# Down projection of a ConvGLU in fp32: every activation sum formed a stage earlier, a seventh raw weight tile, and the fourth weight combination in another order

## The chip, the cores and the metric

The kernel runs on one core of a Trainium2 chip. The metric is device time in microseconds (us) for one execution of the whole program; lower is better. The time before is the median of three runs.

## The reference

One decoder layer and a final norm, all in float32. What the change touches is the last part of the layer, the ConvGLU:

```python
h = rms_norm(x, norm2)
g = causal_dwconv(h @ w_gate)            # 3 taps along the tokens
act = silu(g) * (h @ w_up)
x = x + act @ w_down
```

D_MODEL is 2048, D_FF is 5504 (43 blocks of 128), and there are 512 + 8 x 8 = 576 tokens. Before it stand a norm, one wide input projection, three mixers and an output projection; behind it the final norm. The outputs also hold copies of the caches.

## The kernel before, in words

**Products.** TensorE gets each float32 operand as two rounded halves, hi and lo, and one float32 product is three passes: hi by hi, hi by lo, lo by hi (`product`, L945). A weight tile is split by `split_w`: ScalarE makes the hi half (L933), VectorE subtracts it and leaves the lo half (L934). Three hi and three lo tiles rotate.

**Pairs of blocks.** The 576 tokens are two halves of 288. Both the gate/up stage and the down stage take two output blocks at a time as a 2 x 2 scheme with seven products in place of eight (`strassen_steps`). The weights of a pair come in four raw tiles, b11, b12, b22 and b21. Its products come in the order 11, s1, s2, 12, s3, s4, 22. The names are those of the activation operands. The weight operands are b11; b12 - b11 (formed on VectorE, L990); T2 = b22 - that (VectorE, L998); b21; b22 - b12 (VectorE, L1005); b22; and b21 - T2, the fourth combination, formed on GpSimd (L1009) in b21's own tile. In the up stage a product is 24 matmuls with weight tiles of 128 x 1024 (512 KB), in the down stage 15 matmuls with tiles of 128 x 640 (320 KB). After product 11, ScalarE copies its result (L985), so one L985 is one pair. Results are taken from PSUM by VectorE; in the down stage that is L1487, which adds them to the residual x1.

**Raw weight tiles** come from `raw_tile`, which hands out tiles `wr` and `wx` in turn, three of each. A load waits until the last reader of its tile is done. Loads are issued on SyncE's queue (SP) in program order, and what stands behind a load that waits, waits too.

**The down stage** goes over D_FF in four chunks of ten blocks (NDC = 4, DCHUNK = 5 pairs of blocks), and in each over the 16 output blocks in eight pairs. The activation operands of a chunk must be there as hi and lo halves: 11, s2 and s1 together as s12, 12 and 22 together as own, s4 and s3 together as s34. Each is one piece, 20 pieces for a chunk. They are kept in 28 slots, of which a chunk takes 18. The pieces of the next chunk are made while this one runs (`act_pieces`), each after a step that PIECE_DUE lists; steps are counted over the products of the chunk. Pieces that are left over go between the first products of the next chunk.

**Where the sums come from.** s1, s2, s3 and s4 are sums and differences of the two token halves of two activation blocks. For chunk 0 they are formed in the up stage by `sums` (L1265, L1266, L1271), stored, and loaded again by `first_pieces`. For chunks 1 to 3 the raw activation blocks are loaded to tiles `al` (six of them), and `act_pieces` forms the sums on VectorE itself (L1445, L1446, L1452) between the splits (L1443, L1456; ScalarE L1442, L1453, L1455). The last three blocks of D_FF are handled after chunk 3 (`last_pieces`), without pieces of this kind.

Of the kernel before, what the change touches and what calls it, by code (L numbers as in the profile page):

```python
# [16 lines left out]
P = 128  # L17
# [5 lines left out]
HALF = 288  # L23
# [60 lines left out]
def decoder_step(ctx: ExitStack, tc, I, O):  # L84
# [16 lines left out]
    def nm(s):  # L101
        uid[0] += 1
        return f"{s}_{uid[0]}"
# [798 lines left out]
    wxs = ctx.enter_context(ExitStack())  # L902
    wx = [wxs.enter_context(tc.tile_pool(name="weights2", bufs=1, side="right", reuse_waits="tile")), 1024]
    tps = ctx.enter_context(ExitStack())
# [14 lines left out]
    def work(n=TOK):  # L919
        return wk.tile([P, n], F32, tag="wk", bufs=16, padded_shape=[P, EW], name=nm("wk"))  # L920
# [3 lines left out]
    def raw_tile():  # L924
        rawn[0] += 1
        if rawn[0] % 2:
            return wp.tile([P, 1024], F32, tag="wr", name=nm("wr"))
        return wx[0].tile([P, wx[1]], F32, tag="wx", bufs=3, name=nm("wx"))

# [38 lines left out]
    def strassen_steps(load, X, evac, split, n, urgent=False, late=False):  # L968
# [25 lines left out]
        yield  # L994
        b22 = load(1, 1) if late else b22
        b21 = load(1, 0)
# [23 lines left out]
        with first():  # L1020
            hl = split(w, b21[:, :w])
        product(a, hl, c["22"], False)
# [216 lines left out]
    def state_out(nst, f0, nf):  # L1239
# [4 lines left out]
        for f in range(nf):  # L1244
# [4 lines left out]
    sum_d = [(dp.tile([P, TOK], F32, name=f"s12d{i}"), dp.tile([P, TOK], F32, name=f"s34e{i}"))  # L1249
             for i in range(DCHUNK)]  # L1250
# [33 lines left out]

    def first_pieces(X, n):

        half = [work() for _ in range((n + 1) // 2)]
        for i in range(n):
            j = i % 2 * HALF
            dma(half[i // 2][:, j:j + HALF], act_d[2 * i][:, :HALF])  # L1290

        def load(src):
            t = work()
            dma(t, src)
            return t

        raw = {("s12", i): load(sum_d[i][0]) for i in range(n)}
        yield
        for i in range(n):
            if i % 2 == 0:  # L1300
                t11 = next_slot("11")
            hl = single_of(t11, i % 2)
            src = half[i // 2][:, i % 2 * HALF:(i % 2 + 1) * HALF]
            with_unit(nc.scalar.activation(hl[0], src, AF.Copy))
            nc.vector.tensor_sub(hl[1], src, hl[0].bitcast(F32))
            X.put("11", i, hl)
            yield
        todo = [(c, i) for c in ("s12", "own", "s34") for i in range(n)]
        for c, i in todo:
            if c == "own" and i == 0:  # L1310
                raw.update({("own", k): load(act_d[2 * k + 1]) for k in range(n - 1)})
            if c == "own" and i == n - 1:
                raw.update({("own", n - 1): load(act_d[2 * n - 1])})
                raw.update({("s34", k): load(sum_d[k][1]) for k in range(n)})
            t = next_slot(c)
            src = raw[c, i]
            with_unit(nc.scalar.activation(t[:, 0], src, AF.Copy))
            nc.vector.tensor_sub(t[:, 1], src, t[:, 0].bitcast(F32))
            for name, hl in zip({"s12": ("s2", "s1"), "own": ("12", "22"), "s34": ("s4", "s3")}[c], pair_of(t)):
                X.put(name, i, hl)  # L1320
            yield
# [18 lines left out]
    for nf in GROUPS:  # L1340
# [8 lines left out]
        if f0 == 0:  # L1349
            begun = {0: gate_pair(ht, 0, 0, urgent=True), 2: gate_pair(ht, 2, 2, urgent=True, late=True)}  # L1350
            advance(begun[0][2], 3)
            advance(begun[2][2], 2)
        for f in range(0, nf, 2):
            ff = f0 + f
# [21 lines left out]
            if ups and nf > 1:  # L1376
                for _ in up_steps(*ups.pop(0)):
                    pass
                go_on(len(later))
            if f + 1 < nf:  # L1380
# [4 lines left out]

    nextX = Halves(DCHUNK)
    nxt = first_pieces(nextX, DCHUNK)
    steps = up_steps(*ups.pop(0))
    next(steps)
    next(nxt)  # L1390
    free.extend(n_ for k in RELEASE for n_ in rest[k])
    for n_ in FIRST_PIECES:
# [20 lines left out]

    AL = 6

    def act_tile(k):
        t = fp.tile([P, TOK], F32, tag="al", bufs=AL, name=nm("al"))
        dma_paced(t, act_d[k])
        return t

    def act_pieces(X, k0, n):

        al, t11 = [], {}
        order_ = [(c, i) for i in range(n - 2) for c in ("11", "s12", "own", "s34")]
        order_ += [(c, i) for i in (n - 2, n - 1) for c in ("11", "s12")]
        order_ += [(c, i) for c in ("own", "s34") for i in (n - 2, n - 1)]
        names = {(c, i): free.pop(0) for c, i in order_ if c != "11" or i % 2 == 0}
        for (c, _), name in names.items():
            now.setdefault(c, []).append(name)

        def load():
            if len(al) < n:
                i = len(al)
                al.append((act_tile(k0 + 2 * i), act_tile(k0 + 2 * i + 1)))

        def piece(c, i):
            ae, ao = al[i]
            if c == "11":
                if i % 2 == 0:
                    t11[i // 2] = slot_of(names[c, i])  # L1440
                hl = single_of(t11[i // 2], i % 2)
                with_unit(nc.scalar.activation(hl[0], ae[:, :HALF], AF.Copy))  # L1442
                nc.vector.tensor_sub(hl[1], ae[:, :HALF], hl[0].bitcast(F32))  # L1443
                X.put("11", i, hl)
                nc.vector.tensor_add(ae[:, HALF:], ae[:, HALF:], ao[:, HALF:])  # L1445
                nc.vector.tensor_sub(ae[:, :HALF], ae[:, HALF:], ae[:, :HALF])  # L1446
                return
            t = slot_of(names[c, i])
            src = ae if c == "s12" else ao
            if c == "s34":  # L1450
                s2 = ae[:, :HALF].unsqueeze(1).to_broadcast([P, 2, HALF])
                with_unit(nc.vector.tensor_sub(halves(ao), halves(ao), s2))  # L1452
                nc.scalar.activation(t[:, 0], src, AF.Copy)  # L1453
            else:
                with_unit(nc.scalar.activation(t[:, 0], src, AF.Copy))  # L1455
            nc.vector.tensor_sub(t[:, 1], src, t[:, 0].bitcast(F32))  # L1456
            for name, hl in zip({"s12": ("s2", "s1"), "own": ("12", "22"), "s34": ("s4", "s3")}[c], pair_of(t)):
                X.put(name, i, hl)
            if c == "s34":
                load()  # L1460

        for _ in range(AL // 2):
            load()
        yield
        for c, i in order_:
            piece(c, i)
            yield

# [25 lines left out]
    for ci in range(NDC):  # L1494
# [3 lines left out]
        if ci < NDC - 1:  # L1498
            nextX = Halves(DCHUNK)
            nxt = act_pieces(nextX, f0 + nf, DCHUNK)  # L1500
# [7 lines left out]
        for m in range(0, KD, 2):  # L1508
            def load(h, c, m=m, wv=wv):
                t = raw_tile()  # L1510
                last_w[0] = dma(t[:, :DCHUNK * P].rearrange("p (k c) -> p k c", k=DCHUNK), wv[h][:, :, (m + c) * P:(m + c + 1) * P])
                return t
            pairs.append(strassen_steps(load, X, add_to(m), split_w, DCHUNK, urgent=m < 4,
                                        late=m == 2))
        going, last = last, nxt
# [137 lines left out]
```

## Time and profile before

| | us |
|---|---|
| median of 3 runs (lowest, highest) | 2648.74 (2645.61, 2650.98) |
| the profiled execution | 2641.39 |
| its span in the trace | 2639.5 |
| TensorE busy | 2551.3 (97%) |
| VectorE busy | 1920.6 (73%) |
| ScalarE busy | 972.1 (37%) |
| GpSimd busy | 622.8 (24%) |

The profiled execution is 7.35 us under the median. Its span leaves out 1.9 us around the program. Busy shares are means over stages with different limits.

In the rows below, a window row gives its bounds and length in us, then the busy time and the number of instructions of TensorE (PE), its weight loads (PEld), VectorE (DVE), ScalarE (ACT) and GpSimd (POOL), the granted TensorE clock as a share of full speed, the DMA engines' busy share and GB/s. A timeline row gives start and duration in us, engine, line, operation and out<-in, and in brackets how long the engine had been idle before it and what ended that. A chain row gives start and duration of one piece of the chain that ended last. A group row gives busy us, mean ns of one, and idle us before.
 The up stage lies at about 1140 to 2050 us of the span, the down stage's four chunks at about 2080 to 2570 us.

### The profile page before, as it was taken

To read this page: it belongs to the slowest core of one execution; us is meant where nothing else is said; L and a number is where in the kernel's file an instruction comes from. 1 tells how busy PE (TensorE), PEld (TensorE's weight loads), DVE (VectorE), ACT (ScalarE), POOL (GpSimd) and SP (SyncE) were. 2 spreads that over 40 slices of the span, in tenths; PEclk is the share of its full clock that TensorE was granted. 3 is DMA by queue.
4 is the path that set the end of the run, shared out by engine and by line. 5 is a ranking of instruction groups with operands and counts; after the bars stand their busy time and mean duration, and the time that the engine had idled before them with its cause. 6 is when DMAs were issued, how large, how long until landed. Compare 5 with 4: busy or idle time off the path is not lost.

```text
span 2639.5 us, 48741 instructions
## 1 busy us (share of the span) xinstructions
PE 2551.3 (97%) x19855; PEld 2495.6 (95%) x19855; DVE 1920.6 (73%) x2619; ACT 972.1 (37%) x1445; POOL 622.8 (24%) x460
## 2 busy tenths in 40 slices
PE   8999989989999999999999999999999999989997
PEld 7999889989989999999999999999999998989897
DVE  5667766865766544597878787877777888888875
ACT  6121221222121233354444444444444544444445
POOL 0434334434443000022222121212121111101014
PEclk9999989989999999999999999999999999999999
DMA  8547457537655696556555555555555865555534
GB/s 272 140 122 182 134 148 194 164 110 197 167 152 168 179 281 196 162 181 194 172 185 157 177 153 169 161 166 161 169 162 175 286 183 152 148 147 168 160 100 150
DMA packets 608210, 451.47 MB, mean 171 GB/s; under 512 B 22967, under 2 KB 570082, under 8 KB 601586
## 3 DMA queue, kind: packets, MB, share of 16 engines
q1 hardware_dynamic: 591358, 438.72, 56.0%
q10 hardware_dynamic: 16628, 9.64, 1.2%
q8 instruction: 156, 2.56, 0.4%
q14 instruction: 68, 0.56, 0.1%
HBM read 402.75 MB, written 132.81 MB: 203 GB/s over the span
## 4 chain that ended last, share of the span: by engine, by line
PE 83%; DVE 8%; DMA 6%; issue 1%; ACT 1%; SPq 0%; POOL 0%; DVEq 0%; ACTq 0%
PE a L945 27%; PE acc L176 11%; PE acc L178 10%; PE acc L177 10%; PE pt L945 7%; PE s L945 6%; PE b L945 6%; DMA ev<-in_cache_kv_w_dram 2%; DVE wl L934 2%; DMA al<-act 1%; DVE av L594 1%; DVE xs L1456 1%; DMA wr<-in_w_down_dram 1%; DVE wl L153 1%; PE ps L569 1%
## 5 line engine op out<-in xcount | busy, mean ns | idle before, releaser
L945 PE MATMUL a<-xs,wh 128*128 128x288 f32 x4032 | 814.4, 296 | 14.2 <-ACT wh L933 8.4
L945 PEld LDWEIGHTS a<-xs,wh 128*128 128x128 f32 x4032 | 647.7, 189 | 21.0 <-ACT wh L933 10.7
L176 PE MATMUL acc<-xs,wh 128*128 128x288 f32 x2208 | 663.4, 301 | 0.0
L177 PE MATMUL acc<-xs,wh 128*128 128x288 f32 x2208 | 657.1, 298 | 0.4 <-DVE xs L203 0.3
L178 PE MATMUL acc<-xs,wl 128*128 128x288 f32 x2208 | 655.9, 297 | 0.2 <-DVE wl L153 0.2
L945 PE MATMUL a<-xs,wl 128*128 128x288 f32 x2016 | 592.6, 295 | 1.6 <-DVE wl L934 1.6
L933 ACT ACTIVATE wh<-wr 128x1024 fp32r<-128x1024 f32 (+1 forms) x300 | 276.7, 924 | 519.7 <-PE a L945 210.9
L176 PEld LDWEIGHTS acc<-xs,wh 128*128 128x128 f32 x2208 | 417.5, 189 | 8.4 <-issue 7.6
L178 PEld LDWEIGHTS acc<-xs,wl 128*128 128x128 f32 x2208 | 419.5, 190 | 4.4 <-issue 3.9
L177 PEld LDWEIGHTS acc<-xs,wh 128*128 128x128 f32 x2208 | 418.5, 190 | 1.7 <-DVE xs L200 0.6
L945 PEld LDWEIGHTS a<-xs,wl 128*128 128x128 f32 x2016 | 378.5, 188 | 2.9 <-DVE wl L934 2.7
L1009 POOL TENSOR_TENSOR wx<-wx,wr 128x1024 f32<-128x1024 f32 (+1 forms) x75 | 161.7, 2157 | 883.3 <-DVE wl L934 747.7
L152 ACT ACTIVATE wh<-wr 128x1024 fp32r<-128x1024 f32 (+1 forms) x150 | 155.4, 1037 | 581.7 <-PE acc L177 505.3
L934 DVE TENSOR_TENSOR wl<-wr,wh 128x1024 fp32r<-128x1024 f32 (+1 forms) x300 | 316.1, 1055 | 73.1 <-ACT wh L933 70.0
L934 DVE TENSOR_TENSOR wl<-wx,wh 128x1024 fp32r<-128x1024 f32 (+1 forms) x225 | 273.8, 1223 | 84.7 <-ACT wh L933 84.5
L153 DVE TENSOR_TENSOR wl<-wr,wh 128x1024 fp32r<-128x1024 f32 (+1 forms) x150 | 242.7, 1619 | 105.5 <-ACT wh L152 99.1
L933 ACT ACTIVATE wh<-wx 128x1024 fp32r<-128x1024 f32 (+1 forms) x225 | 206.5, 921 | 169.7 <-PE b L945 85.9
L945 PE MATMUL s<-xs,wh 128*128 128x288 f32 x1024 | 208.0, 295 | 0.0
L945 PE MATMUL b<-xs,wh 128*128 128x288 f32 x1008 | 206.7, 296 | 0.3
L945 PE MATMUL pt<-xs,wh 128*128 128x288 f32 x992 | 203.1, 297 | 3.7 <-ACT wh L933 3.7
L499 POOL TENSOR_TENSOR eq<-qb,ek 128x1024 f32<-128x1024 f32 x48 | 123.1, 2565 | 224.7 <-DMA ek<-in_cache_kv_w_dram 104.4
L499 POOL TENSOR_TENSOR prod<-qb,ek 128x1024 f32<-128x1024 f32 x48 | 122.7, 2557 | 189.6 <-PE acc L176 102.6
(321 smaller groups left out, 3662.5 us busy)
## 6 DMA issues: line engine op xcount, KB each, us to landing
out_dram<-in_cache_kv_w_dram SPq DMA_DIRECT2D x320, 204.0 KB
wr<-in_w_in_dram SPq DMA_DIRECT2D x110, 512.0 KB
ek<-in_cache_kv_w_dram SPq DMA_DIRECT2D x52, 512.0 KB
ev<-in_cache_kv_w_dram SPq DMA_DIRECT2D x52, 512.0 KB
wx<-in_w_gate_dram SPq DMA_DIRECT2D x43, 512.0 KB
wr<-in_w_gate_dram SPq DMA_DIRECT2D x43, 512.0 KB
wr<-in_w_up_dram SPq DMA_DIRECT2D x43, 512.0 KB
wx<-in_w_up_dram SPq DMA_DIRECT2D x43, 512.0 KB
```

The costliest lines, as they stand in the source:

```text
L152: nc.scalar.activation(hi[:, :n], dst, AF.Copy)
L153: low.tensor_sub(lo[:, :n], dst, hi[:, :n].bitcast(F32))
L176: mark.append(nc.tensor.matmul(o, wh, xh, start=first, stop=False))
L177: nc.tensor.matmul(o, wh, xl, start=False, stop=False)
L178: nc.tensor.matmul(o, wl, xh, start=False, stop=last)
L499: with_unit(nc.gpsimd.tensor_mul(pv_, c["q"], keys))
L569: nc.tensor.matmul(o[32 * j:32 * j + 32, :P], pm[:, c:c + 32], rhs, start=i < 4, stop=i >= len(terms) - 4, tile_position=(0, 32 * j), skip ...
L594: i_ = nc.vector.scalar_tensor_tensor(av[:, t, :], v[:, t, :], w, av[:, t, :], op0=ALU.mult, op1=ALU.add)
L933: nc.scalar.activation(hi[:, :n], src, AF.Copy)
L934: nc.vector.tensor_sub(lo[:, :n], src, hi[:, :n].bitcast(F32))
L945: mm = nc.tensor.matmul(o, a[:, ws], b, start=first and k == 0 and i == 0, stop=k == n - 1 and i == 2, skip_group_check=True)
L1009: nc.gpsimd.tensor_sub(b21[:, :w], b21[:, :w], b11[:, :w])
```

## The change

Five things change.

1. `sums` now runs for all 20 pairs of blocks in the up stage, not only for the first five, and stores both results (288 KB each) to DRAM.
2. `act_pieces` is written anew and used for chunk 0 also. It only splits: each of the 20 pieces has one ScalarE and one VectorE instruction. It loads operands instead of blocks, 20 loads for a chunk (5 of 144 KB, 15 of 288 KB) in place of 10 of 288 KB. The `al` tiles are five instead of six. The order of pieces is 11 five times, then s12, own and s34, and PIECE_DUE has 17 entries that are spread evenly (the first is the loads); four s34 pieces are left for the next chunk's first steps.
3. The down stage has seven raw weight tiles, three `wr` and four `wx`. The gate/up stage keeps six.
4. The fourth combination is written over T2 in b11's tile, so it waits for T2's split, and product 22 reads it from there; b21's tile comes free with it, and b11's only after product 22's split. This holds in both stages.
5. In the down stage the third pair no longer loads b22 late, and the first pair is carried one step further before the loop; two more steps of the first gate pairs are taken early, and one call that runs work held back is gone.

```diff
-PIECE_DUE = (4, 8, 12, 16, 19, 22, 25, 28, 31, 34, 37, 40, 46, 47, 47, 48, 49, 50, 51)
+PIECE_DUE = (2, 5, 8, 11, 14, 17, 20, 23, 27, 31, 35, 39, 42, 45, 46, 48, 50)
...
-        if rawn[0] % 2:
+        if rawn[0] % (wx[2] + 3) in (1, 3, 5):
...
-        nc.gpsimd.tensor_sub(b21[:, :w], b21[:, :w], b11[:, :w])
+        nc.gpsimd.tensor_sub(b11[:, :w], b21[:, :w], b11[:, :w])
...
-            hl = split(w, b21[:, :w])
+            hl = split(w, b11[:, :w])
         product(a, hl, c["22"], False)
...
-        if ff < 2 * DCHUNK:
+        if ff < 2 * NDC * DCHUNK:
             sums(ff // 2, g1, g2)
...
+    def act_pieces(X, c, tile_, dma_, ahead_):
...
+        todo = [(kind, i) for kind in ("11", "s12", "own", "s34") for i in range(n)]
...
+            dma_(t, {"s12": sum_d[r][0], "own": act_d[k0 + 2 * i + 1], "s34": sum_d[r][1]}[kind])
...
+            with_unit(nc.scalar.activation(d0, src, AF.Copy))
+            nc.vector.tensor_sub(d1, src, d0.bitcast(F32))
...
+            load_to(done_ + ahead_)
             yield
...
-    wx[:] = [ctx.enter_context(tc.tile_pool(name="weights3", bufs=1, side="right", reuse_waits="tile")), DCHUNK * P]
+    wx[:] = [ctx.enter_context(tc.tile_pool(name="weights3", bufs=1, side="right", reuse_waits="tile")), DCHUNK * P, 4]
...
-    AL = 6
+    AL = 5
...
-                nc.vector.tensor_add(ae[:, HALF:], ae[:, HALF:], ao[:, HALF:])
-                nc.vector.tensor_sub(ae[:, :HALF], ae[:, HALF:], ae[:, :HALF])
...
-                with_unit(nc.vector.tensor_sub(halves(ao), halves(ao), s2))
...
+        next(pairs[0])
         for steps in pairs:
```

In the changed kernel L998 is L1000, L1005 is L1007, L1009 is L1011, L1160 (a gate or up weight load) is L1162, L1487 is L1468, and every VectorE split of a piece is L1341.

The first place is VectorE's order at the start of the second chunk; names are out<-in with the tiles' numbers. Before:

```order
L934 TENSOR_TENSOR wl_24220<-wr_24213,wh_24219 128x640
L1487 TENSOR_TENSOR wk_23690<-s_24055,wk_23690 128x288
L1452 TENSOR_TENSOR al_23428<-al_23428,al_23426 128x576
L1456 TENSOR_TENSOR xs_24204<-al_23726,xs_24204 128x576
L990 TENSOR_TENSOR wr_24213<-wx_24215,wr_24213 128x640
L1445 TENSOR_TENSOR al_24422<-al_24422,al_24424 128x288
L1487 TENSOR_TENSOR wk_23688<-a_24027,wk_23688 128x288
L1456 TENSOR_TENSOR xs_24239<-al_23428,xs_24239 128x576
L1005 TENSOR_TENSOR wx_24215<-wr_24217,wx_24215 128x640
L934 TENSOR_TENSOR wl_24246<-wr_24213,wh_24245 128x640
L1452 TENSOR_TENSOR al_23726<-al_23726,al_23724 128x576
L998 TENSOR_TENSOR wr_24213<-wr_24217,wr_24213 128x640
```

And in the changed kernel:

```order
L934 TENSOR_TENSOR wl_24354<-wr_24347,wh_24353 128x640
L990 TENSOR_TENSOR wr_24347<-wx_24349,wr_24347 128x640
L1468 TENSOR_TENSOR wk_23830<-s_24196,wk_23830 128x288
L1341 TENSOR_TENSOR xs_24338<-al_24076,xs_24338 128x576
L1007 TENSOR_TENSOR wx_24349<-wx_24351,wx_24349 128x640
L934 TENSOR_TENSOR wl_24379<-wr_24347,wh_24378 128x640
L1468 TENSOR_TENSOR wk_23828<-a_24168,wk_23828 128x288
L1341 TENSOR_TENSOR xs_24373<-al_24143,xs_24373 128x576
L1000 TENSOR_TENSOR wr_24347<-wx_24351,wr_24347 128x640
```

Between b11's split (the first row) and the split of b12 - b11 there were eight instructions and there are four: the sums L1452 and L1445 and one piece's split (L1456) are gone from there, and one of two residual additions now comes behind.

The second place is SP's queue in the up stage, over one pair of up weights. The act rows store the activations of the pair before, out_dram rows are cache copies. Before (b11, b12, two stores, b21, b22):

```order
L1160 DMA wr_17523<-in_w_up_dram 128x8x128
L1160 DMA wx_17525<-in_w_up_dram 128x8x128
L1256 DMA act_11901<-wk_16547 128x576
L1255 DMA act_11900<-wk_16545 128x576
L1160 DMA wx_17596<-in_w_up_dram 128x8x128
L1160 DMA wr_17527<-in_w_up_dram 128x8x128
L140 DMA out_dram<-in_cache_kv_w_dram 16x3264 x6
L1160 DMA wr_17787<-in_w_gate_dram 128x8x128
```

And in the changed kernel (b12 stands further ahead; then b11, four stores, b21, the next gate pair's b12, and only then b22):

```order
L1162 DMA wr_17588<-in_w_up_dram 128x8x128
L1258 DMA act_11901<-wk_16598 128x576
L1257 DMA act_11900<-wk_16596 128x576
L1269 DMA s12d_11951<-wk_17337 128x576
L1274 DMA s34e_11952<-wk_17419 128x576
L1162 DMA wx_17661<-in_w_up_dram 128x8x128
L140 DMA out_dram<-in_cache_kv_w_dram 16x3264 x5
L1162 DMA wx_17855<-in_w_gate_dram 128x8x128
L1162 DMA wr_17592<-in_w_up_dram 128x8x128
L140 DMA out_dram<-in_cache_kv_w_dram 16x3264
L1162 DMA wr_17853<-in_w_gate_dram 128x8x128
```

b22's load has moved behind five copies and one more weight load. It takes the tile that the pair before held as b11, which now comes free only with that pair's last split.

## Rows read from the trace of the kernel before

**Rows 1.** Windows of the up stage: with sums, and without.
```profile
1254.00:1320.00 66.00, 66.00 (x500) 66.00 (x499) 55.04 (x69) 30.16 (x38) 16.31 (x17) 1.00 0.54 171
1452.00:1518.00 66.00, 66.00 (x501) 66.00 (x500) 48.73 (x57) 27.19 (x36) 12.45 (x11) 1.00 0.58 177
```

**Rows 2.** Windows of the down stage: chunk starts and chunk middles in turn.
```profile
2074.00:2116.00 42.00, 38.76 (x274) 36.38 (x273) 37.55 (x60) 18.85 (x30) 4.12 (x2) 1.00 0.99 332
2116.00:2200.00 84.00, 81.00 (x595) 78.88 (x594) 74.31 (x112) 38.75 (x62) 11.77 (x6) 1.00 0.55 160
2200.00:2243.00 43.00, 37.37 (x253) 36.44 (x252) 33.54 (x54) 14.84 (x23) 3.12 (x2) 0.92 0.56 168
2243.00:2326.00 83.00, 80.00 (x587) 77.78 (x586) 73.22 (x109) 38.21 (x61) 11.71 (x6) 1.00 0.50 146
2326.00:2369.00 43.00, 37.21 (x252) 35.92 (x251) 33.63 (x54) 15.42 (x24) 3.12 (x2) 0.92 0.58 171
2369.00:2452.00 83.00, 80.21 (x590) 78.21 (x590) 73.67 (x110) 37.92 (x60) 11.71 (x6) 1.00 0.49 142
2452.00:2489.00 37.00, 32.33 (x233) 30.81 (x233) 30.07 (x47) 14.57 (x22) 3.15 (x2) 1.00 0.59 194
2489.00:2573.00 84.00, 84.00 (x634) 83.80 (x634) 67.49 (x98) 33.88 (x52) 10.46 (x7) 1.00 0.39 111
```

**Rows 3.** Timeline of ScalarE: first product's copy (L985) in four pairs.
```profile
2243.65 0.38 ACT L985 COPY b<-a 128x288 f32<-128x288 f32 x1 [2.53 <-PE a L945]
2258.00 0.38 ACT L985 COPY b<-a 128x288 f32<-128x288 f32 x1 [2.52 <-PE a L945]
2549.84 0.39 ACT L985 COPY b<-a 128x288 f32<-128x288 f32 x1
...
2563.75 0.39 ACT L985 COPY b<-a 128x288 f32<-128x288 f32 x1
```

**Rows 4.** Timeline of VectorE, end of chunk 0, start of chunk 1.
```profile
2194.17 2.03 DVE L1456 TENSOR_TENSOR xs<-al,xs 128x576 fp32r<-128x576 f32 x1
...
2207.34 0.46 DVE L1445 TENSOR_TENSOR al<-al,al 128x288 f32<-128x288 f32 x1 [1.18 <-DMA al<-act]
...
2209.48 0.82 DVE L934 TENSOR_TENSOR wl<-wr,wh 128x640 fp32r<-128x640 f32 x1
...
2226.17 0.83 DVE L998 TENSOR_TENSOR wr<-wr,wr 128x640 f32<-128x640 f32 x1 [2.77 <-DMA wr<-in_w_down_dram]
```

**Rows 5.** Timeline of TensorE around the same place.
```profile
2210.35 0.40 PE L945 MATMUL pt<-xs,wl 128*128 128x288 f32 x1 [2.38 <-DVE wl L934]
```

**Rows 6.** Timeline of GpSimd, end of chunk 0.
```profile
2194.02 1.57 POOL L1009 TENSOR_TENSOR wx<-wx,wr 128x640 f32<-128x640 f32 x1 [11.78 <-DVE wl L934]
```

**Rows 7.** Timeline of the SP queue, start of chunk 1.
```profile
2204.81 8.28 SPq L140 DMA_DIRECT2D al<-act  x4
```

**Rows 8.** Chain of waits: transfers before and at a chunk's start.
```profile
2083.73 7.38 DMA al<-act
...
2220.98 5.16 DMA wr<-in_w_down_dram
```

**Rows 9.** VectorE groups by form in the down stage.
```profile
L1452 DVE TENSOR_TENSOR al<-al,al 128x576 f32<-128x576 f32 x15 | 11.2, 749 | 1.7 <-PE s L945 1.7
...
L1445 DVE TENSOR_TENSOR al<-al,al 128x288 f32<-128x288 f32 x15 | 8.2, 544 | 7.9 <-DMA al<-act 7.9
L1446 DVE TENSOR_TENSOR al<-al 128x288 f32<-128x288 f32 x15 | 6.5, 446 | 0.0
```

**Rows 10.** Timeline of VectorE in the up stage.
```profile
1515.23 1.22 DVE L934 TENSOR_TENSOR wl<-wx,wh 128x1024 fp32r<-128x1024 f32 x1 [0.56 <-ACT wh L933]
...
1521.38 1.21 DVE L1005 TENSOR_TENSOR wx<-wr,wx 128x1024 f32<-128x1024 f32 x1
...
1522.88 1.22 DVE L934 TENSOR_TENSOR wl<-wr,wh 128x1024 fp32r<-128x1024 f32 x1
```

**Rows 11.** Chain of waits in the up stage.
```profile
1520.54 6.33 PE a L945 x48
```

More of the change, by code (lines that the diff above doesn't have):

```diff
@@ L994, in strassen_steps @@
         yield
-        b22 = load(1, 1) if late else b22
+        if late:
+            b22 = load(1, 1)
+            yield
         b21 = load(1, 0)
@@ L1283, in next_slot @@
         return slot_of(name)
[L1285 to L1297, printed above, removed]
-        yield
[L1299 to L1320, printed above, removed]
@@ new lines, in act_pieces, with load11, load, load_to @@
+    def act_pieces(X, c, tile_, dma_, ahead_):
+        n = DCHUNK
+        k0 = 2 * n * c
+        todo = [(kind, i) for kind in ("11", "s12", "own", "s34") for i in range(n)]
+        names = {}
+        loads = []
+        raw = {}
+        def load11(i):
+            t = tile_()
+            for k in range(i, min(i + 2, n)):
+                part = t[:, (k - i) * HALF:(k - i + 1) * HALF]
+                dma_(part, act_d[k0 + 2 * k][:, :HALF])
+                raw["11", k] = part
+        def load(kind, i):
+            t = raw[kind, i] = tile_()
+            r = n * c + i
+            dma_(t, {"s12": sum_d[r][0], "own": act_d[k0 + 2 * i + 1], "s34": sum_d[r][1]}[kind])
+        for kind, i in todo:
+            if kind != "11":
+                loads.append((kind, i))
+            elif i % 2 == 0:
+                loads.append((kind, i))
+        at_ = 0
+        def load_to(m):
+            nonlocal at_
+            while at_ < min(m, len(loads)):
+                kind, i = loads[at_]
+                load11(i) if kind == "11" else load(kind, i)
+                at_ += 1
+        load_to(ahead_)
+        yield
+        for kind, i in todo:
+            if kind != "11" or i % 2 == 0:
+                names[kind, i] = free.pop(0)
+                now.setdefault(kind, []).append(names[kind, i])
+        for j, (kind, i) in enumerate(todo):
+            src = raw[kind, i]
+            if kind == "11":
+                if i % 2 == 0:
+                    t11 = slot_of(names[kind, i])
+                d0, d1 = single_of(t11, i % 2)
+                X.put("11", i, (d0, d1))
+            else:
+                t = slot_of(names[kind, i])
+                d0, d1 = t[:, 0], t[:, 1]
+                for name, hl in zip({"s12": ("s2", "s1"), "own": ("12", "22"), "s34": ("s4", "s3")}[kind], pair_of(t)):
+                    X.put(name, i, hl)
+            with_unit(nc.scalar.activation(d0, src, AF.Copy))
+            nc.vector.tensor_sub(d1, src, d0.bitcast(F32))
+            del raw[kind, i]
+            done_ = loads.index((kind, i - i % 2 if kind == "11" else i)) + (kind != "11" or i % 2 or i + 1 == n)
+            load_to(done_ + ahead_)
@@ L1386, in decoder_step @@
     nextX = Halves(DCHUNK)
[L1387 removed]
+    nxt = act_pieces(nextX, 0, work, dma, 8)
     steps = up_steps(*ups.pop(0))
     next(steps)
+    free.extend(n_ for k in RELEASE for n_ in rest[k])
     next(nxt)
[L1391 removed]
     for n_ in FIRST_PIECES:
@@ L1412, in next_raw, with al_tile @@
         return (sl2 if name.startswith("x2") else sl).tile([P, n], F32, tag=name, name=nm("fo"))
-    AL = 6
+    AL = 5
+    def al_tile():
+        return fp.tile([P, TOK], F32, tag="al", bufs=AL, name=nm("al"))
     def act_tile(k):
-        t = fp.tile([P, TOK], F32, tag="al", bufs=AL, name=nm("al"))
+        t = al_tile()
         dma_paced(t, act_d[k])
         return t
[L1421 to L1444, printed above, removed]
-                nc.vector.tensor_add(ae[:, HALF:], ae[:, HALF:], ao[:, HALF:])
-                nc.vector.tensor_sub(ae[:, :HALF], ae[:, HALF:], ae[:, :HALF])
[L1447 to L1451, printed above, removed]
-                with_unit(nc.vector.tensor_sub(halves(ao), halves(ao), s2))
[L1453 to L1467, printed above, removed]
@@ L1512, in load @@
                 return t
-            pairs.append(strassen_steps(load, X, add_to(m), split_w, DCHUNK, urgent=m < 4,
-                                        late=m == 2))
+            pairs.append(strassen_steps(load, X, add_to(m), split_w, DCHUNK, urgent=m < 4))
         going, last = last, nxt
```

12 lines of the change are left out of this document (7 added, 5 removed).

## The prediction

> **What bounds the kernel now.** I read the windows first, since busy shares over the whole span mix stages. In the up stage TensorE is busy for all of a 66 us window, with 500 or 501 matmuls, whether VectorE is busy for 48.73 us or, where the sums of the first five pairs are formed, for 55.04 us [rows 1]. So the up stage has no time to give, and it has shown that it can carry the sums. The down stage is different. Its last chunk, which makes almost no pieces, also runs without a gap: 634 matmuls in 84.00 us, 0.1325 us each [rows 2]. I take that as the full rate. A pair there takes 2563.75 - 2549.84 = 13.91 us [rows 3], which is 7 x 15 x 0.1325. All other stretches of the down stage hold fewer matmuls than fit. Their loss is length less matmuls times 0.1325, by the rows in turn: chunk 0's start 42 - 274 x 0.1325 = 5.7; middles 5.2, 5.2 and 4.8; starts of chunks 1 to 3 9.5, 9.6 and 6.1 [rows 2]. That is 46.1 us in all: 15.2 in the middles, 25.2 at the three starts, 5.7 at the first. The granted clock at two starts is 0.92, between its levels of 1.2 and 2.4 GHz, and 1.00 in the middles; it is under 1.00 only in stretches in which TensorE had stood still, and I count it as part of the same loss.
>
> What ends the waits there? At the start of chunk 1 a matmul of product s1 waits 2.38 us for a weight's lo half from VectorE [rows 5]. That split (L934, 2209.48) runs late, since VectorE, which works in order, had stood 1.18 us before the sum L1445 at 2207.34 until raw activations landed, and had other piece work beside [rows 4]. A few products later VectorE stands 2.77 us before T2 (L998, 2226.17), for a weight transfer [rows 4] that the chain shows from 2220.98 for 5.16 us [rows 8]. It was issued late, because the SP queue spent 8.28 us from 2204.81 on four activation loads that waited for tiles [rows 7]. So the starts lose time to sums, to the raw loads that they wait for, and to weight loads stuck behind these.
>
> **The change part by part.**
>
> *Sums leave the down stage.* Per chunk 5 x (749 + 544 + 446) ns = 8.7 us of VectorE go [rows 9], and with them two dependences: ScalarE's split waiting for a sum, and the sum waiting for raw blocks. In the middles VectorE falls from 74.31 us in 84 [rows 2] by roughly six eighths of 8.7, to 67.8. The last chunk has 67.49 there and loses nothing [rows 2]. Yet one thing stays: a pair with only plain pieces, such as that from 2243.65 to 2258.00, takes 14.35 us against 13.91 [rows 3], 0.44 more. A piece's split can take 2.03 us where GpSimd's combination runs beside it [rows 4, 6]; the plain one of equal shape takes 749 ns [rows 9]. I take 6 x 0.45 = 2.7 us as what a middle goes on losing (bounds: 0, as the last chunk, and 5.1, as now). Gain: 15.2 - 3 x 2.7 = 7.1 us (0 to 15.2).
>
> *Starts of chunks 1 to 3.* Before, seven pieces were due in the last six steps before a start, and two behind it; now six over the last twelve, and four s34 pieces behind, which product s3 is the first to need. Between b11's split and the next one stand four instructions on VectorE instead of eight, and the one piece among them reads a tile that was loaded five pieces ahead. Ahead of T2 the weights have a seventh tile. I leave each start three pairs of 0.45 and 0.65 us for the four late pieces' splits, about 2 us: gain 25.2 - 6 = 19.2 us. Bounds: 0, if new waits take the place, and 25.2.
>
> *Start of chunk 0.* As many pieces as before are made behind the up stage's last products, and as many are left for the chunk's first steps; only their order of loading is another. The transfers are crowded here, with a DMA share of 0.99 [rows 2] and activation loads that take 7.38 us in the chain [rows 8]. None of that is removed. I take 1.2 of 5.7 us (0 to 5).
>
> *Sums enter the up stage.* 15 pairs x three operations; priced by their like in the down stage that is 15 x 1.74 = 26 us of VectorE [rows 9]. The cover is VectorE's own slack there: 66 - 48.73 = 17.3 us in 66, and a window of 66 us holds one and a half pairs of sums, 2.6 us. The window with sums shows TensorE still full [rows 1]. Cost 0; without the cover, 26 us. The 30 more stores of 288 KB go where the DMA share is 0.54 to 0.58 [rows 1], and the loads, some 2.2 MB more a chunk, where it is 0.49 to 0.59 behind the first stretch [rows 2]: nothing for either, since no stretch comes near the 0.99 that the same queues reached.
>
> *The fourth combination over T2.* GpSimd has it done earlier in a pair, and product 22 waits no longer than before. b11's tile is held from T2's split to the split of product 22 instead. In the up stage this binds: b22's load takes the tile that the pair before held as b11, and so can start only when that split ends, 1515.23 + 1.22 = 1516.45. Its first reader is L1005 at 1521.38 [rows 10], 4.9 us later. Behind L1005 VectorE has the split at 1522.88 [rows 10], which ends at 1524.10 and serves product s1, which TensorE starts at 1520.54 + 6.33 = 1526.87 [rows 11]. So there are 2.8 us more, 7.7 in all. No row shows such a load timed by itself. The nearest are 5.16 us for 320 KB among others and 7.38 us in the most crowded stretch [rows 8]. Both fit within 7.7, so I take 0. At the last it is tight.
>
> *The lock between GpSimd and VectorE.* The combination now starts after T2's split and not after b21's, so it can meet b21's split on VectorE. It met other instructions before: 2.03 against 0.749 us, 1.3 us lost [rows 4, 9]. I take no difference (bounds: 32 pairs x 1.3 = 42 us either way if each meeting stopped TensorE, which the middles, with 0.44 a pair, do not bear out). The Trainium skill, page "SBUF — State Buffer", section "SBUF: two separate sides", says that a GpSimd instruction and a VectorE instruction with two SBUF inputs exclude each other for a whole instruction, whoever starts first. The 2.03 us beside GpSimd's 1.57 us [rows 4, 6] agree. By that rule the loss is whole where GpSimd is first, and the sum would be 2621 + 42 = 2663 us, if it is so in every pair and TensorE waits each time; where VectorE is first, it is nothing, and the sum stands.
>
> Sum: 7.1 + 19.2 + 1.2 = 27.5 us. The profiled execution would go from 2641.39 to 2613.9. It lies 7.35 us under the median of the runs, 2648.74; I take the gain off the median: **2621.2 us**.
>
> **The rivals.**
>
> *A. All chunks run like the last one.* For it: 67.8 us of VectorE in 84 against 67.49 where nothing is lost [rows 2]. Against: the 14.35 us pair. Gain 15.2 + 25.2 + 4 = 44, 2604 us.
>
> *B. The starts recover only in part.* For it: twenty loads a chunk instead of ten share the SP queue with weights, and each waits for one of five tiles; the 8.28 us of SP [rows 7] could come back at another place, and the four pieces left over still precede s3. At half the starts' loss and a third of the middles': 12.6 + 5 = 17.6 less 3 us of new queueing, gain 14, 2634 us.
>
> *C. The collision moves to a worse place.* b21's split feeds the product after next; if GpSimd gets in front of it and TensorE waits for 0.25 us in each of 32 pairs (of the 1.3 at most), 8 us are lost: 2629 us. Above 27.5 / 32 = 0.86 us a pair it would eat the whole gain.
>
> *D. Slower: b22 comes late in the up stage.* The place is L1005 and the split behind it, in each of the 42 gate and up pairs (21 of each from 43 blocks). It decides from 7.7 us between the free tile and the landing; also against it is the queue, where b22 now stands behind five copies. At 9 us, 1.3 x 42 = 55 us are lost against 27.5 gained: about 2676 us. For it speaks the 7.38 us at 0.99 DMA share; against it the share of 0.54 to 0.58 in the up stage [rows 1].
>
> *E. Nothing to measure.* New waits at the starts equal the old, and middles are bound by the pieces' splits: 2644 to 2654 us.
>
> **How the numbers follow.** My forecast 0.50, A 0.18, B 0.12, C 0.08, D 0.07, E 0.05. The likeliest is 2621 us. Leaving out D, E and the fast end of A leaves some 0.2 outside 2603 to 2638 us. 0.2% of the time, 5.3 us, is about what a measurement of this kernel can tell from no change. Faster by more than this: the first four, 0.88; within it: E, 0.05; slower: D, 0.07.
>
> **What would show it.** Right: windows of the up stage with about 500 matmuls in 66 us; chunk middles with 610 or more in 84 us; starts with 300 or more in 43 us at a granted clock near 1.00; no wait of VectorE for `al` and none of T2 for weights. A shows as 634 in 84 us everywhere. Wrong, and by D: fewer than 500 matmuls in 66 us of the up stage and L1007 waiting for the transfer of `wr`. Wrong, and by B: SP rows of `al` loads that hold for several us, and T2 waiting for weights at the starts. Wrong, and by C: a wait of TensorE for L934 in product 12, with GpSimd's L1011 in front of it.

## The result, and the profile after

The changed kernel takes 2617.16 us (median of 4 runs, 2613.19 to 2621.39) beside 2647.18 us of the kernel before: a ratio of 0.9885, 95% interval 0.9865 to 0.9906. The prediction was 2621.2 us. The profiled execution takes 2613.19 us with a span of 2611.4, that is 28.1 us less than the span before.

The windows of the changed kernel, bounded by its own chunk starts and middles, answer to [rows 2]; the columns are the same.

```profile
2119.81:2204.57 84.76, 84.01 (x632) 83.55 (x631) 74.14 (x110) 40.14 (x64) 11.83 (x6) 1.00 0.68 206
2204.57:2235.18 30.61, 29.44 (x212) 28.07 (x211) 26.17 (x39) 13.14 (x22) 3.64 (x2) 1.00 0.63 181
2235.18:2319.93 84.75, 84.01 (x632) 83.54 (x631) 74.14 (x110) 40.13 (x63) 11.88 (x6) 1.00 0.62 191
2319.93:2350.55 30.62, 29.43 (x212) 28.07 (x211) 26.26 (x39) 13.15 (x22) 3.60 (x2) 1.00 0.62 180
2350.55:2435.30 84.75, 84.00 (x632) 83.54 (x631) 74.14 (x110) 40.13 (x64) 11.84 (x6) 1.00 0.63 186
```

A middle now holds 632 matmuls in 84.76 us where 639.7 would fit at full rate: 1.0 us lost in place of 5. The window lies between two of the marks below; six pairs are only 630 matmuls, so two belong to the edges, and by the marks 1.3 us are lost. A start loses 30.61 - 212 x 0.1325 = 2.5 us. The granted clock is 1.00 in these starts and middles; it was 0.92 at two starts. VectorE is busy for the same share of a middle as before (74.14 us of 84.76, 74.31 of 84; 67.8 was predicted): the sums are gone from it, but the same six pairs now take 84.76 us where they took 89.20.

The windows of the up stage answer to [rows 1].

```profile
1254.00:1320.00 66.00, 66.00 (x500) 66.00 (x499) 56.26 (x71) 29.46 (x39) 18.89 (x17) 1.00 0.56 172
1452.00:1518.00 66.00, 65.84 (x497) 65.62 (x497) 55.30 (x64) 27.19 (x36) 15.01 (x11) 1.00 0.62 191
1595.00:1661.00 66.00, 64.56 (x486) 64.11 (x485) 55.43 (x65) 26.82 (x36) 17.50 (x14) 1.00 0.61 185
```

TensorE no longer fills every window: 497 and 486 matmuls. The waits of the changed kernel from 1124 to 2065 us name a new one, for b22 (waiting engine and line, what it waited for, us in total, times, longest):

```profile
DVE wx L1007 <- DMA wr<-in_w_up_dram: 20.5, 15, 3.7
DVE wx L1007 <- DMA wr<-in_w_gate_dram: 7.0, 7, 1.5
```

**Where the time came from.** L985 marks every pair, so the same marks can be compared in all kernels. Four stretches, each between two marks: the up stage is 42 pairs from the first mark; the start of chunk 0 is the next three marks; a start is the first two pairs of a chunk (27.83 us at full rate, 14 x 15 x 0.1325); a middle is the six pairs after it (83.48). One value of a stretch can be followed in the marks of the changed kernel's ScalarE timeline:

```profile
2119.81 0.38 ACT L985 COPY b<-a 128x288 f32<-128x288 f32 x1 [2.76 <-PE a L945]
...
2204.57 0.38 ACT L985 COPY b<-a 128x288 f32<-128x288 f32 x1 [1.17 <-PE a L945]
...
2235.18 0.38 ACT L985 COPY b<-a 128x288 f32<-128x288 f32 x1 [2.76 <-PE a L945]
```

The middle of chunk 0 is 2204.57 - 2119.81 = 84.76 us, the start of chunk 1 2235.18 - 2204.57 = 30.61. In all kernels, us (starts of chunks 1, 2 and 3; middles of chunks 0, 1 and 2; one profiled execution each):

| kernel | up stage | start 0 | starts | middles | span |
|---|---|---|---|---|---|
| before | 937.50 | 54.15 | 37.30, 37.51, 34.61 | 89.20, 89.31, 88.85 | 2639.5 |
| changed | 940.75 | 55.19 | 30.61, 30.61, 31.29 | 84.75, 84.75, 84.75 | 2611.4 |
| e1 old combination in up stage | 937.93 | 55.57 | 30.62, 30.59, 31.31 | 84.76, 84.74, 84.74 | 2613.6 |
| e2 six tiles | 940.73 | 59.12 | 34.49, 33.17, 36.37 | 93.84, 90.21, 89.55 | 2651.0 |
| e3 sums only | 937.52 | 57.62 | 31.09, 32.97, 31.24 | 86.32, 86.49, 85.99 | 2620.5 |
| e4 seventh tile, no sums | 937.56 | 54.55 | 34.16, 35.21, 32.84 | 89.09, 89.36, 88.94 | 2633.1 |
| e5 seven tiles, old combination | 937.99 | 53.17 | 29.32, 29.32, 30.01 | 84.68, 84.68, 84.68 | 2603.4 |
| e6 sums twice | 937.66 | 54.96 | 30.61, 30.60, 31.28 | 84.73, 84.76, 84.73 | 2608.5 |
| e7 bunched pieces | 937.03 | 56.26 | 32.45, 33.97, 33.36 | 86.51, 85.53, 84.44 | 2623.7 |
| e8 no fourth combination | 937.44 | 53.49 | 29.33, 29.33, 30.00 | 83.49, 83.49, 83.49 | 2603.0 |
| e9 fourth on VectorE | 937.92 | 52.33 | 29.50, 29.71, 30.18 | 83.72, 83.73, 83.71 | 2598.2 |
| e10 as e5, again | 937.97 | 53.21 | 29.32, 29.32, 30.01 | 84.67, 84.68, 84.68 | 2606.7 |
| e11 changed, again | 941.43 | 55.60 | 30.60, 30.60, 31.28 | 84.76, 84.73, 84.75 | 2617.3 |
| e12 seventh tile, no sums, old combination | 936.97 | 54.93 | 34.48, 33.50, 33.40 | 88.74, 89.06, 88.94 | 2629.3 |

The stretches repeat to 0.7 us in the up stage, 0.4 at chunk 0's start and 0.1 elsewhere (e10 and e5, e11 and the changed kernel). The spans also hold what lies ahead of the first mark, which scatters by up to 6.8 us over all kernels and by 4.9 between the two runs of the changed one. From before to changed the middles give 13.1 us, the starts 16.9; the up stage costs 3.2 and chunk 0's start 1.0. The rest, 2.4 us, lies before, behind and in the last chunk.

### The profile page after: what moved, and what is told of

The parts are those of the page before. It is cut to its first block, busy times and chain, and to the rows that moved or that the text cites. A ratio compares the mean times of both kernels' runs of the same rounds, so it can differ in the third digit from the quotient of the medians.

```text
span 2611.4 us, 48947 instructions
## 1 busy us (share of the span) xinstructions
PE 2539.8 (97%) x19855; PEld 2488.7 (95%) x19855; DVE 1961.5 (75%) x2619; ACT 966.6 (37%) x1445; POOL 661.5 (25%) x460
## 4 chain that ended last, share of the span: by engine, by line
PE 79%; DVE 9%; DMA 7%; issue 2%; ACT 1%; SPq 1%; POOL 0%; DVEq 0%; ACTq 0%
PE a L945 26%; PE acc L176 10%; PE acc L178 10%; PE acc L177 10%; PE b L945 7%; PE pt L945 6%; PE s L945 6%; DMA ev<-in_cache_kv_w_dram 2%; DVE wl L934 2%; DVE av L594 1%; DVE wl L153 1%; DMA wr<-in_w_up_dram 1%; DMA wr<-in_w_gate_dram 1%; ACT wh L933 1%; PE ps L569 1%
## 5 line engine op out<-in xcount | busy, mean ns | idle before, releaser
L933 ACT ACTIVATE wh<-wr 128x1024 fp32r<-128x1024 f32 (+1 forms) x312 | 298.9, 960 | 499.6 <-PE a L945 163.9
L934 DVE TENSOR_TENSOR wl<-wr,wh 128x1024 fp32r<-128x1024 f32 (+1 forms) x312 | 351.2, 1127 | 60.4 <-ACT wh L933 59.2
L152 ACT ACTIVATE wh<-wr 128x1024 fp32r<-128x1024 f32 (+1 forms) x150 | 155.4, 1037 | 583.0 <-PE acc L177 526.5
L1011 POOL TENSOR_TENSOR wr<-wx,wr 128x1024 f32<-128x1024 f32 (+1 forms) x52 | 157.0, 3019 | 767.5 <-DVE wl L934 687.2
L153 DVE TENSOR_TENSOR wl<-wr,wh 128x1024 fp32r<-128x1024 f32 (+1 forms) x150 | 243.8, 1626 | 102.2 <-ACT wh L152 99.9
L934 DVE TENSOR_TENSOR wl<-wx,wh 128x640 fp32r<-128x640 f32 (+1 forms) x213 | 248.0, 1169 | 38.6 <-ACT wh L933 36.7
L933 ACT ACTIVATE wh<-wx 128x640 fp32r<-128x640 f32 (+1 forms) x213 | 183.2, 865 | 148.3 <-PE a L945 36.8
```

The source lines that it names most:

```text
L152: nc.scalar.activation(hi[:, :n], dst, AF.Copy)
L153: low.tensor_sub(lo[:, :n], dst, hi[:, :n].bitcast(F32))
L933: nc.scalar.activation(hi[:, :n], src, AF.Copy)
L934: nc.vector.tensor_sub(lo[:, :n], src, hi[:, :n].bitcast(F32))
L1011: nc.gpsimd.tensor_sub(b11[:, :w], b21[:, :w], b11[:, :w])
```

## The experiments

**e1: the old combination in the gate and up stage.** The changed kernel with

```diff
-        nc.gpsimd.tensor_sub(b11[:, :w], b21[:, :w], b11[:, :w])
+        b4 = b11 if n == DCHUNK else b21
+        nc.gpsimd.tensor_sub(b4[:, :w], b21[:, :w], b11[:, :w])
...
-            hl = split(w, b11[:, :w])
+            hl = split(w, b4[:, :w])
```

> The changed kernel, but in the gate and up stage the fourth combination is again written to b21's tile; the down stage keeps it over T2. Theory (b22's load, held by b11's tile, costs the up stage its 3 us): no wait of the b22 - b12 subtraction for a transfer in the up stage, the pair marks there back at 22.26 us each, the span 2.5 to 3.5 us shorter, about 2614 us. Rival (the sums' VectorE work costs it): the waits for the transfer go but the marks stay 3 us behind, 2617 us.

2610.61 us, ratio 0.9875 (0.9859 to 0.9891). The up stage is back at 937.93 us and no wait for `wr` is left at the b22 - b12 subtraction; VectorE still forms all sums there. So the 3 us came from b11's longer hold, as the theory says. The span, 2613.6, is not below 2611.4, since the first mark comes 4.6 us later here. How the wait looks in the changed kernel, on VectorE:

```profile
1613.90 1.23 DVE L1007 TENSOR_TENSOR wx<-wr,wx 128x1024 f32<-128x1024 f32 x1 [3.73 <-DMA wr<-in_w_up_dram]
```

and in the chain of the same place, the transfer that it waited for, with the split that had freed its tile:

```profile
1604.20 1.22 DVE L934 TENSOR_TENSOR wl<-wr,wh 128x1024 fp32r<-128x1024 f32 x1 [0.83 <-ACT wh L933]
...
1604.79 9.02 DMA wr<-in_w_up_dram
```

This load took 9.02 us from its issue. The first 0.6 us of them the tile was still being read; from the end of the split, at 1605.42, to the landing at 1613.81 are 8.4 us, more than the 7.7 that the prediction gave it. This is the stretch with 486 matmuls. But of 22 waits, 27.5 us in all on VectorE, few reached TensorE, whose matmuls waited for 2.0 us in all in the up stage.

**e2, e3: the seventh tile, and the sums by themselves.** e2 is the changed kernel with six tiles, e3 also has the old combination in both stages:

```diff
-... side="right", reuse_waits="tile")), DCHUNK * P, 4]
+... side="right", reuse_waits="tile")), DCHUNK * P, 3]
```

> The changed kernel with six raw weight tiles in the down stage (three wx) and all else kept. Theory (the sums and their raw loads were what the chunks lost): each chunk loses 1 to 3 us more than with seven tiles, 2620 to 2626 us. Rival (the weights' supply was): T2 and the b22 - b12 subtraction wait for weight loads in every pair, 4 us or more a pair start, 2635 us or more.

> The changed kernel with six raw weight tiles in the down stage and the fourth combination in b21's tile in both stages, so that the sums, the new pieces and their order are what is left of the change. Theory (sums are the gain): 2614 to 2622 us, middles of a chunk within 2 us of full rate, starts within 4 us. Rival (weights' supply): starts still lose 9 us each to weight loads, 2635 us or more.

e2: 2654.42 us, ratio 1.0037 (1.0022 to 1.0052): slower than before. e3: 2623.20 us, ratio 0.9922 (0.9907 to 0.9937). For e2 the rival's time came out, for e3 the theory's, a little over its 2622. The two go together once the waits are read. In e2 from 2115 to 2460 us:

```profile
DVE wx L1007 <- DMA wr<-in_w_down_dram: 28.9, 19, 3.1
...
DVE wr L1000 <- DMA wr<-in_w_down_dram: 7.4, 2, 3.9
```

and e3's of the same stretch:

```profile
DVE wx L1007 <- DMA wr<-in_w_down_dram: 8.2, 9, 1.6
DVE wr L1000 <- DMA wr<-in_w_down_dram: 6.7, 3, 2.7
```

With six tiles, b11 held until product 22's split makes b22 late in most pairs. In the down stage a product is only 15 matmuls long, where it is 24 in the up stage; that this is why it hides less there is argued, not shown. With seven tiles these rows are gone from the changed kernel's waits. So the combination over T2 needs the seventh tile; it isn't what the tile needs.

**e4, e12: the other half of the change without the sums.** Both are the kernel before with seven tiles, five `al` tiles and no late b22; e4 with the combination over T2 in the down stage, e12 with the old one. The `late` that goes is that of output blocks 2 and 3, so of the second pair of a chunk and not of the third.

```diff
-    AL = 6
+    AL = 5
...
-            pairs.append(strassen_steps(load, X, add_to(m), split_w, DCHUNK, urgent=m < 4,
-                                        late=m == 2))
+            pairs.append(strassen_steps(load, X, add_to(m), split_w, DCHUNK, urgent=m < 4))
```

> The kernel before with the other half of the change: seven raw weight tiles in the down stage, the fourth combination over T2 in the down stage alone, b22 of the third pair not late, five al tiles as the room demands (so two pairs of blocks loaded ahead instead of three). Theory (sums are the gain): 2640 to 2652 us, sums still wait for raw blocks at the starts. Rival (weights' supply): the starts recover two thirds of their 25 us, about 2632 us.

> The kernel before with seven raw tiles in the down stage, the old combination, no late b22 in the third pair and five al tiles: the run without the sums' change, now without the combination over T2 too. Theory (the seventh tile alone gave that run its gain): starts 34 us and span about 2632 us as in that run, or 1 us less at a start. Rival (tile and combination were needed together there): starts about 36.5 us, span about 2640 us.

e4: 2633.60 us, ratio 0.9957 (0.9943 to 0.9972). e12: 2632.22 us, ratio 0.9953 (0.9936 to 0.9969). On average the starts recover 2.4 us each in e4 and 2.7 in e12, less than half of what the changed kernel recovers (5.6), and the middles next to nothing (89.1, 88.9). So for e4 the truth lies between theory and rival, near the rival's time and far from its starts; for e12 the theory holds in that the combination gave e4 nothing. That the tile alone gave the gain is not shown, since both kernels also load the second pair's b22 with its other weights. That pair lies in the start, and this b22 is the load for which T2 stood 2.77 us in the kernel before [rows 4, 8]; TensorE stood for the hi half of that T2:

```profile
2227.90 1.06 PE L945 MATMUL a<-xs,wh 128*128 128x288 f32 x4 [2.09 <-ACT wh L933]
```

In e12 no wait of this kind is left there. No run has the tile with the late load, nor six tiles and the old sums without it. The waits of e12 from 2110 to 2465 us show what stays with the sums:

```profile
PE a L945 <- DVE wk L1489: 6.6, 12, 1.0
...
DVE al L1447 <- DMA al<-act: 5.5, 6, 1.3
```

TensorE waits for residual additions on VectorE, and the sums wait for raw activations.

**e5: seven tiles and the old combination in both stages.** The fourth combination's two lines are those of the kernel before, all else is the changed kernel.

> The changed kernel with seven raw tiles in the down stage, but the fourth combination in b21's tile in both stages. Theory (the seventh tile is what lets the chunks run; over T2 the combination only frees b21's tile early and holds b11's): within 2 us of the run that had the old combination in the up stage alone, a middle about 84.8 us by the marks and a start about 30.6, span 2613 to 2615 us. Rival (tile and combination are needed together): like the run with the sums alone, middles 86.3 and starts 31 to 33 us, span about 2620 us.

2606.27 us, ratio 0.9870 (0.9849 to 0.9890). The span, 2603.4, is 10 us under e1's, beyond both expectations; 4.0 of them lie ahead of the first mark. The middles are as the theory has them, the starts better: 29.32 us against 30.61. So over T2 the combination costs 1.3 us at each start of chunks 1 to 3. The reason stands in the timelines at the start of chunk 1. In the changed kernel GpSimd:

```profile
2207.81 2.08 POOL L1011 TENSOR_TENSOR wr<-wr,wr 128x640 f32<-128x640 f32 x1 [13.96 <-DVE wl L934]
```

VectorE beside it:

```profile
2208.38 2.12 DVE L1341 TENSOR_TENSOR xs<-al,xs 128x576 fp32r<-128x576 f32 x1
2210.42 0.81 DVE L990 TENSOR_TENSOR wx<-wr,wx 128x640 f32<-128x640 f32 x1
```

and TensorE, at product s1:

```profile
2212.12 0.53 PE L945 MATMUL s<-xs,wh 128*128 128x288 f32 x2 [0.61 <-ACT wh L933]
```

The piece's split takes 2.12 us instead of 0.75, so b12 - b11 (L990) comes late, its hi half too, and s1 waits; this wait is 0.6 of the 1.3 us. In e5's second run, e10, at the same place VectorE is done with it before GpSimd starts at 2212.29:

```profile
2207.43 0.75 DVE L1341 TENSOR_TENSOR xs<-al,xs 128x576 fp32r<-128x576 f32 x1
2208.10 0.82 DVE L990 TENSOR_TENSOR wx<-wr,wx 128x640 f32<-128x640 f32 x1
```

**e6: the sums twice.** e1 with every sum operation done twice:

```diff
+            for _ in range(2):
-            nc.vector.tensor_add(a[:, HALF:], g1[:, HALF:], g2[:, HALF:])
-            nc.vector.tensor_sub(a[:, :HALF], a[:, HALF:], g1[:, :HALF])
+                nc.vector.tensor_add(a[:, HALF:], g1[:, HALF:], g2[:, HALF:])
+                nc.vector.tensor_sub(a[:, :HALF], a[:, HALF:], g1[:, :HALF])
...
```

> The kernel with the old combination in the up stage alone, and there each of the three sum operations of all 20 pairs done twice (the second leaves the same values): 60 more VectorE operations, about 33 us by 0.55 us each. Theory (VectorE's slack covers the sums in the up stage): the pair marks in the up stage stay at 22.26 us, its length 937.9 us within 1 us. Rival (the cover is nearly used up): 5 us or more longer.

2609.74 us, ratio 0.9881 (0.9860 to 0.9901); up stage 937.66 us, as without. Sixty more VectorE operations cost nothing there.

**e7: the pieces bunched at the end.** e1 with

```diff
-PIECE_DUE = (2, 5, 8, 11, 14, 17, 20, 23, 27, 31, 35, 39, 42, 45, 46, 48, 50)
+PIECE_DUE = (4, 8, 12, 16, 19, 22, 25, 28, 31, 34, 37, 46, 47, 47, 48, 49, 50)
```

> The kernel with the old combination in the up stage alone, with the pieces' due steps bunched towards the end of a chunk as before the change: six of the seventeen in the last five steps, where evenly spread ones have three. Theory (what the starts regained came from the sums and raw loads that went, not from the spread): starts lose at most 1 us more, span within 3 us of 2613.6. Rival (the spread regained it): starts go back by 3 us or more each, middles gain up to 1 us each, span about 2620 us or more.

2625.09 us, ratio 0.9937 (0.9920 to 0.9954). The theory falls: starts lose 1.8, 3.4 and 2.1 us more, and the middles 1.8, 0.8 and nothing, so that about 10 us of the changed kernel's gain hang on the spread by the stretches, and 15 by the medians on one chip (e6, which is like e1 in time, has 2609.74). The rival had the time right, but not the middles, which lose instead of gaining. The chain of waits shows how, at the start of chunk 1:

```profile
2202.10 5.49 DMA al<-s34e
2207.61 0.69 ACT xs L1341
```

With pieces close together their loads are too, and a split waits for one that has only been issued.

**e8: no fourth combination in the down stage.** e1 with

```diff
+        if n != DCHUNK:
-        nc.gpsimd.tensor_sub(b4[:, :w], b21[:, :w], b11[:, :w])
+            nc.gpsimd.tensor_sub(b4[:, :w], b21[:, :w], b11[:, :w])
```

> The kernel with the old combination in the up stage alone, and in the down stage no fourth combination at all: product 22 takes T2 as its weights, so that the output lacks that part. It shows what the meeting of GpSimd and VectorE costs. Theory (what a middle still loses is this meeting): middles from 84.75 to about 83.5 us by the marks, splits of wx tiles from a mean of 0.9 to 0.82 us, span 2 to 6 us shorter. Rival (it is the pieces' own splits): middles stay within 0.4 us.

One execution took 2604.82 us, span 2603.0. That is 10.6 us less than e1 and more than expected, since the starts gain 1.3 us each and chunk 0's start 2.1 too. The middles are 83.49 us, full rate within 0.03. So all that a middle still loses is GpSimd's meeting with VectorE, and pieces' splits cost TensorE nothing. The groups of VectorE from 2110 to 2460 us (busy us, mean ns) for e8, where GpSimd does nothing:

```profile
L934 DVE TENSOR_TENSOR wl<-wx,wh 128x640 fp32r<-128x640 f32 x101 | 82.2, 821 | 21.2 <-ACT wh L933 20.6
...
L1343 DVE TENSOR_TENSOR xs<-al,xs 128x576 fp32r<-128x576 f32 x45 | 33.8, 750 | 0.4
```

and for the changed kernel:

```profile
L934 DVE TENSOR_TENSOR wl<-wx,wh 128x640 fp32r<-128x640 f32 x99 | 89.5, 912 | 18.9 <-ACT wh L933 18.3
...
L1341 DVE TENSOR_TENSOR xs<-al,xs 128x576 fp32r<-128x576 f32 x45 | 40.4, 898 | 0.4
```

**e9, e10, e11: the fourth combination on VectorE, and a comparison on one chip.** e9 is e5 with

```diff
-        nc.gpsimd.tensor_sub(b21[:, :w], b21[:, :w], b11[:, :w])
+        eng = nc.vector if n == DCHUNK else nc.gpsimd
+        eng.tensor_sub(b21[:, :w], b21[:, :w], b11[:, :w])
```

> The kernel with seven tiles and the old combination in both stages, and in the down stage the fourth combination on VectorE in place of GpSimd: 32 more VectorE instructions of about 0.82 us, 26 us. Theory (what the middles still lose is GpSimd's meeting with VectorE, and a middle has VectorE slack for 6 x 0.82 us): middles from 84.68 to about 83.5 us, starts 29.3, 3 to 4 us faster than the same kernel with GpSimd. Rival (VectorE's queue in order then puts splits late at the starts, where it is fullest): starts back to 31 us or more, no gain or slower.

> The kernel with seven tiles and the old combination in both stages once more, beside the changed kernel on one chip. Theory (over T2 the combination costs 3 us in the up stage and 1.3 us at each of four starts of a chunk): 7 to 9 us faster than the changed kernel, ratio to before 0.985. Rival (the difference between earlier runs was the chip's): within 3 us of the changed kernel.

> The changed kernel itself once more, as the other side of that comparison: ratio to before 0.9885 as first measured, up stage 940.7 us by the marks, starts 30.6 us.

e9: 2603.41 us, ratio 0.9848 (0.9830 to 0.9867). e10: 2609.93 us, 0.9868 (0.9852 to 0.9884). e11: 2619.26 us, 0.9905 (0.9888 to 0.9921). With the old combination the kernel is 9.3 us faster than the changed one, a little over what was expected. With the combination on VectorE the middles fall to 83.7 us, and the starts lose only 0.2 to 0.4 us. By the stretches that is 2.9 us in the middles less 0.7 at the starts, and 0.9 at chunk 0's start: 3.1 us, and 0.8 more in the last chunk. The 6.5 us between the medians are more, but the two intervals overlap, so no more than these 3 to 4 us is shown. e9 is the fastest kernel here, 16 us under the changed one.

## Why the prediction came out

**Right: what bounds.** The chunks' loss was where the windows put it, and it went: 46.1 us of it were counted, 30 came back in chunks 1 to 3's starts and the middles.

**The starts: size right, cause incomplete.** 19.2 us were predicted, 16.9 came. The prediction gave the gain to the sums and their raw loads with a tile ahead of T2. The runs part it in two. By the ratios, which hold the whole kernel, the sums' half (e3) gives 0.78%, the seventh tile without the sums (e12) 0.47%, both together with the old combination (e10) 1.32%: near to the sum. All three also load the second pair's b22 in time, which the prediction did not price. The even PIECE_DUE, which the prediction counted but did not price, holds 10 us or more of the sums' half (e7 against e1).

**The middles: too small a gain.** 7.1 us were predicted, 13.1 came. The step that failed is "a pair with only plain pieces ... 0.44 more", carried to all pairs as 0.45. Its cause, a piece's split beside GpSimd's combination, was rightly named, but in most pairs the meeting does not reach TensorE: it waits for the split of b21 in two of a middle's six pairs (the row for C below), and a middle loses 1.3 us and not 2.7. e8 shows that the 1.3 are this meeting alone. Here rival A was near: without GpSimd's instruction the middles do run as the last chunk. Not for the reason that it gave, though. The 67.8 us of VectorE in 84 were too low: the window of 84 us that they come from held 595 of the 630 matmuls of six pairs, so that its 74.31 us make an estimate of 78.7 for a middle before. The changed kernel's VectorE is busy for 74.14 us in a middle, well above the last chunk's 67.49 [rows 2], and only 1.3 us are lost.

**The up stage: predicted 0, cost 3.** The sums are free there, as argued, twice over (e6). The step that failed is "Both fit within 7.7, so I take 0": b22's load was seen to take 9.02 us, 8.4 from the free tile, with five copies ahead of it on the queue. The rows that it leaned on were of smaller transfers; the 5.16 us for 320 KB [rows 8], scaled by size alone, would have been an estimate of 8.3 us for 512 KB. Rival D's place and mechanism were right, its price was not: 55 us were worked out as if every pair lost its excess. VectorE waited 27.5 us, yet TensorE lost 3 us over 42 pairs; it waits for a lo half at product s1 once, for 0.9 us.

**The lock: predicted no difference, cost 1.3 us at each start.** "I take no difference" failed; the order of the two engines' instructions decides what is hit. Over T2, GpSimd starts while pieces' splits and the next pair's b12 - b11 are in the queue behind. The rule of the Trainium skill, page "SBUF — State Buffer", section "SBUF: two separate sides", that such instructions exclude each other whole, agrees with 2.12 against 0.75 us, and with the mean of 750 ns for all 45 pieces once GpSimd is still. C's place, the split of b21 before product 12, shows too in TensorE's waits of the changed kernel from 2115 to 2460 us:

```profile
PE b L945 <- DVE wl L934: 2.2, 6, 0.5
```

In e10 this row is gone and another stands in its place, for residual additions at other products, and the middles are equal (84.75 and 84.68):

```profile
PE a L945 <- DVE wk L1468: 1.9, 3, 0.6
```

So in the middles the collision only moved, as predicted; at the starts it did not.

**Chunk 0's start: predicted to gain 1.2, lost 1.0.** The loss lies between its first and second mark, here in the kernel before and in the changed one:

```profile
2083.45:2092.84 9.39, 7.68 (x49) 6.65 (x49) 8.14 (x14) 5.62 (x10) 0.00 (x0) 1.00 1.06 387
2084.91:2097.99 13.08, 8.91 (x49) 7.75 (x47) 9.61 (x14) 5.53 (x9) 2.01 (x1) 0.87 1.04 370
```

It takes 3.7 us longer, of which the next stretch gives 2.5 back. In the changed kernel VectorE stands there for a residual load that is late, and TensorE for the lo half behind it:

```profile
2091.01 0.46 DVE L1468 TENSOR_TENSOR wk<-pt,wk 128x288 f32<-128x288 f32 x1 [3.47 <-DMA wk<-x1d]
...
2092.26 0.61 PE L945 MATMUL a<-xs,wl 128*128 128x288 f32 x1 [2.67 <-DVE wl L934]
```

The granted clock over this stretch, 1.00 before, is 0.87, between its levels of 1.2 and 2.4 GHz. e5 loses nothing at this start (53.2), but whether that is due to the combination is open: e1 has the same 13.08 us without the residual's wait, and e8, which has no fourth combination, takes 11.42 us at a clock of 0.85. The stretch takes 9.4 to 10.3 us in the five kernels whose clock stays at 1.00 in it (before, e2, e5, e9, e10) and 10.4 to 13.5 in all others, at 0.84 to 0.87.

The four terms add to 13.1 + 16.9 - 3.2 - 1.0 = 25.8 us, where 27.5 were predicted: what the middles gave beyond the forecast, 6.0, was taken back by the starts (2.3), the up stage (3.2) and chunk 0's start (2.2). The time came out close by luck, because these errors cancel, not because each term was right.

## What to carry to other kernels

Work taken from a stage that is short of an engine and given to one with slack is worth the stalls that it made, not its busy time: some 26 us of sums, moved out with their raw loads and with the pieces spread evenly, gave 22 us back (e3), about 10 of them by the spread as e7 has it, and cost nothing where they went. When a tile's last reader moves, follow every load that inherits the tile: the same edit cost 3 us where a product lasts 24 matmuls and made the kernel slower than before where it lasts 15 and no tile was added. And an instruction put on an idle engine can stop a busy one: 32 combinations of 0.82 us are cheaper by 3 to 4 us on a busy VectorE than on a mostly idle GpSimd.

## What the runs showed of the hardware that was not expected

A weight transfer of 512 KB took 9.02 us from issue to landing with the DMA engines busy for 0.61 of the time in the window around it, more than the 7.38 us seen for 288 KB where they were busy for 0.99: a share far from 0.99 did not make it short. Whether its size or the five copies ahead of it made it long, no run parts. GpSimd's subtraction of 128 x 640 took from 1.57 us in the kernel before to 2.78 in e10, VectorE's 0.82 (e9), and while GpSimd's ran VectorE's split of 0.75 us took 2.12. In the changed kernel, granted clock under 1.00 vanished from the starts of chunks 1 to 3 with the stalls, and came up at chunk 0's start (0.87); no run shows by itself what it costs.
